# Where experts with several items stand in the loading order of a mixture-of-experts step

## The chip, the cores and the metric

The kernel runs on one core of a Trainium2 chip. The metric is the device time of one execution in microseconds (us), median of three runs. Engines are named as in the profile: PE (TensorE matmul; PEld its weight loads), DVE (VectorE), ACT (ScalarE), POOL (GpSimd), SP (SyncE, which here only issues transfers and waits). SPq marks rows of SP's queue. "L137" is line 137 of the kernel.

## The reference

One decoder layer for 512 prompt tokens and 8 x 4 sample tokens, in float32: an input projection, two mixers (a matrix-memory recurrence and sliding-window attention), a merge, and a hierarchical mixture of experts, then a gated per-layer embedding, each with a layer norm. The change touches only how the experts are scheduled. Cut to that part:

```python
def hier_moe(x, ...):
    g_idx = argmax(x @ w_rg + b_rg)                 # 1 of 4 groups
    top_p, top_i = top_k(softmax(e_logits of that group), 2)   # 2 of its 8 experts
    gate = g_w * top_p / top_p.sum()
    eid = g_idx * 8 + top_i
    y[tok] += gate * (silu(x @ w_gate[eid]) * (x @ w_up[eid])) @ w_down[eid]

x = layer_norm(ALPHA * x + hier_moe(x, ...))
```

There are 32 experts. Each has a gate and an up matrix of 1024 x 512 and a down matrix of 512 x 1024, 2 MiB each, so 6 MiB for one expert. 544 tokens with two experts each make 1088 rows. With the inputs of the reference they fall on 26 of the 32 experts: 230 rows on the fullest, one row on the emptiest.

## The kernel before

**Items and places.** The rows of an expert are cut into items of up to 32 rows. The 26 experts have 49 items: 18 experts have one item, two have 2, three have 3, two have 5 and one has 8. An expert's position in the loading order is its place (0 to 25). PE works through the items in the order of places; SP loads the weights in the same order.

**The order of loading.** It is worked out on the chip, from the counts of rows, by a key for each expert (lines 2037 to 2053); experts are then ranked by the key (lines 2057 to 2080), and the places, the items up to each place and the ends are written to `meta` (L2100). Four experts (ranks 16 to 19 of a list made early from the biases) are loaded before the routing is known; `firsts` holds 32 for them, and their key is about -32, so they take places 0 to 3. Among the other experts in use, `kinds[:, 0]` marks those of exactly one item (S = 14 here) and `kinds[:, 1]` those of more (M = 8 here). `nth` numbers each kind from 1 in the order of the experts' indices. The n-th of the single-item experts has the key n - 0.5; the m-th of the others has the key m x `ratio`, with `ratio` = S / (M + 1) = 14 / 9 = 1.556, which is called the distance here. `ties` adds less than 0.01. An unused expert gets 1000 more.

**Buffers.** There are four slots for weights. Slots 0 and 1 are tiles that the profile calls `w`; slot 2 is `w2a`, `w2b` (the two halves of gate and up) and `w2c`, `w2d` (down); slot 3 is `gu3a`, `gu3b` and `r_p`. Place p uses slot p mod 4 for p up to 23; the last two, 24 and 25, use slots 2 and 3, and slots 0 and 1 are left to what comes behind the experts.

**SP (from L179).** `load_place` (L137, L143) loads a place in six transfers of 1 MiB, in this order: gate and up, first half, when PE has done the first half of gate and up of the last item that uses the slot; gate and up, second half, when PE has done the second half; the two halves of down, when PE has done the down product of that item. SP goes through the places strictly in order, so a wait for one slot holds back all that stands behind it. For places 24 and 25 it waits for places 22 and 23. Behind the experts come the `late` loads (L230): four of 512 KiB (`x1d`) and one of 2 MiB (`w_pg`), which `act` waits for at the end of the phase (semaphore `al`).

**PE (`items_of`).** For each item: 64 matmul instructions for gate and up (L306), in two halves that wait for the two halves of the weights, and then 32 for the down product (L318) of the item before it. So the last down product of a place comes behind the gate and up of the next place. Behind every fourth item PE also turns the next 128 gathered rows (L298). ACT and DVE make silu(gate) x up (L440, L515) and turn it (L479); POOL gathers the rows and scatters the results (L256, L265).

Of the kernel before, what the change touches and what calls it, by code (L numbers as in the profile page):

```python
# [15 lines left out]
ALU = mybir.AluOpType  # L16
# [528 lines left out]
def tile_decoder_step(ctx: ExitStack, tc: tile.TileContext, *aps):  # L545
    nc = tc.nc
    A = dict(zip(_INS + _CONSTS + _OUT_NAMES, aps))
    sy, act, dve, pe, gp = nc.sync, nc.scalar, nc.vector, nc.tensor, nc.gpsimd
# [125 lines left out]
    for pp in range(2):  # L674
        gp.dma_start(
            out=brow[16 + 4 * pp:20 + 4 * pp, :].rearrange("j (a d) -> j a d", a=2),
# [1260 lines left out]
    with ExitStack() as scope:  # L1937
# [26 lines left out]
        def rt(name, shape, dt=F32):  # L1964
            n = -(-count(shape) // 8) * 8
            if dt != F32 or taken[0] + n > arena.shape[1]:
                return R.tile(shape, dt, name=name)
            taken[0] += n
            return view(arena[:, taken[0] - n:taken[0] - n + count(shape)], shape)
# [21 lines left out]
        items, flag, base, key = (rt(n, [P, NEXP]) for n in ("items", "flag", "base", "key"))  # L1991
# [43 lines left out]
        kinds, nth = rt("kinds", [P, 2, NEXP]), rt("nth", [P, 2, NEXP])  # L2035
        ratio = rt("ratio", [P, 1])
# [12 lines left out]
        dve.scalar_tensor_tensor(out=key, in0=nth[:, 0], scalar=-0.5, in1=kinds[:, 0], op0=ALU.add, op1=ALU.mult)  # L2049
        dve.tensor_tensor(out=ratio, in0=ratio, in1=nth[:, 0, NEXP - 1:], op=ALU.mult)  # L2050
        dve.tensor_tensor(out=base, in0=base, in1=key, op=ALU.add)
        dve.scalar_tensor_tensor(out=key, in0=nth[:, 1], scalar=ratio, in1=kinds[:, 1], op0=ALU.mult, op1=ALU.mult)
        dve.tensor_tensor(out=key, in0=key, in1=base, op=ALU.add)

        E = NEXP
        sq, kcol, bcol_ = rt("sq", [E, E]), rt("kcol", [E, 1]), rt("bcol", [E, 1])
# [36 lines left out]
        for n, by, op, m_ in ((80, K["turns"][0:1], ALU.add, 16), (82, iota[0:1, 0:32], ALU.mult, 32)):  # L2093
# [4 lines left out]
                                 op0=ALU.mult, op1=ALU.subtract)  # L2098
# [10 lines left out]
                          in1=hi[:, :, None].to_broadcast([P, 2 * NT5, 20]), op=ALU.is_equal)  # L2109
# [357 lines left out]
```

## Time and profile before

| what | us |
|---|---|
| median of three runs | 1088.85 |
| lowest and highest run | 1086.99, 1091.53 |
| profiled execution, own time | 1091.46 |
| its span (first to last instruction) | 1089.6 |
| PE / DVE / ACT / POOL busy in the span | 995.5 / 510.3 / 367.0 / 253.8 |

The profiled execution lies 2.6 us above the median, and 1.9 us of its time lie outside its span. Up to about 630 us the span holds the projection, the mixers and the merge; the expert phase runs from about 637 to 1012 us; what follows is the tail (second and third norm, gated embedding, outputs). How to read what the prediction quotes: a row of the timeline has start, duration, engine, line, operation, tiles, the count of instructions merged into it, and in brackets the idle time of the engine before it with what ended it. "Issue" there means that the profile shows nothing the engine waited for. A row of the windows has a stretch of the span, its length, the busy time of PE, PEld, DVE, ACT and POOL with the number of instructions, the granted PE clock, the busy share of the 16 DMA engines and the GB/s that they moved.

The items can be counted in the trace: 1408, 384 and 480 instructions of L306 read `w`, `w2a` and `gu3a`. An item has 64 on `w` (both halves of its weights are called so) or 32 on each of `w2a` and `gu3a`, which makes 22 + 12 + 15 = 49 items.

### The profile page before, as it was taken

To read this page: it belongs to the slowest core of one execution; us is meant where nothing else is said; L and a number is where in the kernel's file an instruction comes from. 1 tells how busy PE (TensorE), PEld (TensorE's weight loads), DVE (VectorE), ACT (ScalarE), POOL (GpSimd) and SP (SyncE) were. 2 spreads that over 40 slices of the span, in tenths; PEclk is the share of its full clock that TensorE was granted. 3 is DMA by queue.
4 is the path that set the end of the run, shared out by engine and by line. 5 is a ranking of instruction groups with operands and counts; after the bars stand their busy time and mean duration, and the time that the engine had idled before them with its cause. 6 is when DMAs were issued, how large, how long until landed. Compare 5 with 4: busy or idle time off the path is not lost.

```text
span 1089.6 us, 26983 instructions
## 1 busy us (share of the span) xinstructions
PE 995.5 (91%) x10269; PEld 818.1 (75%) x10270; DVE 510.3 (47%) x1308; ACT 367.0 (34%) x749; POOL 253.8 (23%) x385
## 2 busy tenths in 40 slices
PE   9999999999999999999999976885988788987897
PEld 8988999999988888899989544553556565655675
DVE  5556533635756865664465721211222222223796
ACT  5311223532596784423211311110111111113531
POOL 6000000501445564213410211111222222221011
PEclk9999999999999999999999988999899999999899
DMA  7221322223515432645289989999999999969811
GB/s 260 79 78 42 114 64 67 70 77 96 162 41 151 142 127 98 229 116 151 84 320 381 364 317 409 427 426 426 427 426 426 425 427 426 426 265 420 318 45 63
DMA packets 90892, 256.45 MB, mean 235 GB/s; under 512 B 11115, under 2 KB 58433, under 8 KB 70820
## 3 DMA queue, kind: packets, MB, share of 16 engines
q1 hardware_dynamic: 76036, 224.61, 53.5%
q0 software_dynamic: 10272, 27.21, 6.9%
q10 hardware_dynamic: 4512, 3.64, 1.2%
q8 instruction: 49, 0.80, 0.3%
q14 instruction: 23, 0.19, 0.1%
HBM read 241.89 MB, written 19.61 MB: 240 GB/s over the span
## 4 chain that ended last, share of the span: by engine, by line
PE 49%; issue 6%; DMA 5%; SPq 4%; DVE 3%; ACT 1%; POOL 0%; DVEq 0%; ACTq 0%; POOLq 0%
PE psG L306 14%; PE pj L709 6%; PE kept L318 6%; PE pj L710 6%; PE pj L711 6%; SPq L137 3%; DMA gu3b<-in_w_eu_dram 2%; DMA w<-in_w_pg_dram 2%; PE psX L298 1%; SPq L143 1%; PE po L711 1%; PE sp L1397 1%; PE po L709 1%; PE po L710 1%; PE nm L1385 1%
## 5 line engine op out<-in xcount | busy, mean ns | idle before, releaser
L709 PE MATMUL pj<-xH,wH 128*128 128x256 f32 (+1 forms) x672 | 197.9, 295 | 0.3 <-ACT sigA L879 0.3
L710 PE MATMUL pj<-xL,wH 128*128 128x256 f32 (+1 forms) x672 | 195.9, 292 | 0.0
L711 PE MATMUL pj<-xH,wL 128*128 128x256 f32 (+1 forms) x672 | 194.4, 290 | 0.0
L592 ACT CAST wH<-raw 128x1024 fp32r<-128x1024 f32 x76 | 79.6, 1048 | 192.8 <-PE pj L710 119.0
L709 PEld LDWEIGHTS pj<-xH,wH 128*128 128x128 f32 x672 | 126.5, 188 | 5.9 <-issue 4.4
L711 PEld LDWEIGHTS pj<-xH,wL 128*128 128x128 f32 x672 | 126.4, 188 | 1.4 <-issue 1.2
L710 PEld LDWEIGHTS pj<-xL,wH 128*128 128x128 f32 x672 | 126.4, 188 | 1.3 <-issue 0.8
L593 DVE TENSOR_TENSOR wL<-raw,wH 128x1024 fp32r<-128x1024 f32 x76 | 95.8, 1261 | 66.2 <-ACT wH L592 66.1
L474 DVE COPY xT<-xg 128x256 f32 x48 | 14.5, 302 | 228.4 <-PE psG L306 228.4
L306 PE MATMUL psG<-w,xT 128*32 128x256 f32 x1408 | 89.9, 412 | 31.2 <-issue 30.3
L306 PEld LDWEIGHTS psG<-w,xT 128*32 128x32 f32 x1408 | 55.2, 118 | 63.6 <-issue 44.3
L440 ACT ACTIVATE both<-psG 128x128 f32<-128x128 f32 x49 | 13.6, 278 | 245.5 <-PE psG L306 245.4
L1373 POOL TENSOR_SCALAR lg<-lg,sm 128x256 f32<-128x256 f32 (+1 forms) x64 | 60.0, 951 | 26.2 <-DVE sm L1370 19.9
L265 POOL DMA_INDIRECT ybuf<-ysb,idy x48 | 47.8, 995 | 43.6 <-POOL idy L262 31.6
L426 ACT ACTIVATE xg<-psX,gcol 128x128 f32 (+1 forms) x100 | 36.4, 469 | 50.5 <-PE psX L298 50.5
L709 PE MATMUL pj<-wH,xH 128*128 128x256 f32 x160 | 46.7, 292 | 1.1 <-DVE vs L923 1.0
L318 PE MATMUL kept<-w,hT 128*32 128x256 f32 x704 | 42.5, 379 | 2.5 <-DVE hT L479 2.5
L306 PE MATMUL psG<-gu3a,xT 128*32 128x256 f32 x480 | 30.7, 398 | 15.3 <-issue 6.8
L710 PE MATMUL pj<-wL,xH 128*128 128x256 f32 x160 | 44.3, 277 | 0.0
L711 PE MATMUL pj<-wH,xL 128*128 128x256 f32 x160 | 44.3, 277 | 0.0
L479 DVE STREAM_TRANSPOSE hT<-both 128x128 f32<-128x128 f32 x49 | 20.0, 409 | 44.1 <-PE kept L318 43.8
L253 POOL COPY idx<-tok 128x1 int32 (+1 forms) x12 | 2.2, 185 | 159.4 <-PE psX L298 159.4
(655 smaller groups left out, 2280.8 us busy)
## 6 DMA issues: line engine op xcount, KB each, us to landing
w<-in_w_eg_dram SPq DMA_DIRECT2D x24, 1024.0 KB
w<-in_w_eu_dram SPq DMA_DIRECT2D x24, 1024.0 KB
w<-in_w_ed_dram SPq DMA_DIRECT2D x24, 1024.0 KB
raw<-in_w_in_dram SPq DMA_DIRECT2D x22, 1024.0 KB
r_p<-in_w_ed_dram SPq DMA_DIRECT2D x14, 1024.0 KB, 22.5
w2a<-in_w_eg_dram SPq DMA_DIRECT2D x7, 1024.0 KB
w2a<-in_w_eu_dram SPq DMA_DIRECT2D x7, 1024.0 KB
w2b<-in_w_eg_dram SPq DMA_DIRECT2D x7, 1024.0 KB
```

The lines of the kernel that those rows point to most:

```text
L137: return [eng.dma_start(out=W[s][half][:, i], in_=w[i][bass.ds(e, 1)].rearrange("a (p k) f -> (a p) k f", p=P)[:, ks]) for i in range(2)]
L265: gp.indirect_dma_start(out=ybuf.rearrange("t (q d) -> (t q) d", q=4), out_offset=bass.IndirectOffsetOnAxis(ap=idy[:, r:r + 1], axis=0), i ...
L306: m = pe.matmul(psG[32 * q:32 * q + 32], xT[:, k], W[s][half][:, :, kh, P * q:P * q + P], start=k == 0, stop=k == KD - 1)
L318: m = pe.matmul(out[32 * q:32 * q + 32], hT[:, 32 * k:32 * k + 32], W[s][2][k // 2][:, k % 2, 256 * q:256 * q + 256], start=k == 0, stop=k ...
L426: m = act.activation(out=out, in_=psX[:, k], func=AF.Identity, bias=gcol[:, 1, k:k + 1], scale=gcol[:, 0, k:k + 1])
L479: dve.transpose(out=hT[:].rearrange("p (r t) -> p r t", r=4), in_=h[:].rearrange("p (f r) -> p r f", r=4)).then_inc(S["ch"], 1)
L592: act.copy(out=H, in_=src)
L593: return eng.tensor_tensor(out=L, in0=src, in1=H.bitcast(F32), op=ALU.subtract)
L709: pe.matmul(out, lh(k), rh(k), start=start and i == 0, stop=False)
L710: pe.matmul(out, lh(k), rl(k), start=False, stop=False)
L711: pe.matmul(out, ll(k), rh(k), start=False, stop=stop and i == len(ks) - 1)
L1373: gp.tensor_scalar(out=lg[:, par, j, 0:nk], in0=lg[:, par, j, 0:nk], scalar1=sm[:, 2, par, j:j + 1], scalar2=None, op0=ALU.mult)
```

## The change

```diff
         dve.tensor_tensor(out=base, in0=base, in1=key, op=ALU.add)
-        dve.scalar_tensor_tensor(out=key, in0=nth[:, 1], scalar=ratio, in1=kinds[:, 1], op0=ALU.mult, op1=ALU.mult)
-        dve.tensor_tensor(out=key, in0=key, in1=base, op=ALU.add)
+        dve.scalar_tensor_tensor(out=key, in0=nth[:, 1], scalar=-1.0, in1=kinds[:, 1], op0=ALU.add, op1=ALU.mult)
+        dve.scalar_tensor_tensor(out=key, in0=key, scalar=ratio, in1=base, op0=ALU.mult, op1=ALU.add)
```

The m-th expert of several items gets the key (m - 1) x ratio instead of m x ratio; nothing else changes. With S = 14 and M = 8 the keys of these eight are 0, 1.556, ... 10.889 instead of 1.556, 3.111, ... 12.444, while the single-item experts keep 0.5, 1.5, ... 13.5. The number of items at each place follows from the keys:

| place | 0-3 | 4 | 5 | 6 | 7 | 8 | 9 | 10 | 11 | 12 | 13 | 14 | 15 | 16 | 17 | 18 | 19 | 20 | 21 | 22 | 23 | 24 | 25 |
|---|---|---|---|---|---|---|---|---|---|---|---|---|---|---|---|---|---|---|---|---|---|---|---|
| before | 1 each | 1 | 1 | 2 | 1 | 3 | 1 | 1 | 8 | 1 | 3 | 1 | 1 | 3 | 1 | 5 | 1 | 1 | 5 | 1 | 2 | 1 | 1 |
| after | 1 each | 2 | 1 | 1 | 3 | 1 | 8 | 1 | 1 | 3 | 1 | 3 | 1 | 1 | 5 | 1 | 5 | 1 | 1 | 2 | 1 | 1 | 1 |

The expert of eight items moves from place 11 (slot 3) to place 9 (slot 1), the two of five items from 18 and 21 to 17 and 19, and the last expert of two items from 23 to 22.

## The prediction

> **What bounds the kernel now.** The page's busy times come first, and its rates of transfer (40 slices of 27.2 us).
>
> ```profile
> PE 995.5 (91%) x10269; PEld 818.1 (75%) x10270; DVE 510.3 (47%) x1308; ACT 367.0 (34%) x749; POOL 253.8 (23%) x385
> GB/s 260 79 78 42 114 64 67 70 77 96 162 41 151 142 127 98 229 116 151 84 320 381 364 317 409 427 426 426 427 426 426 425 427 426 426 265 420 318 45 63
> ```
>
> PE is busy 91% of the span, which says little of the expert phase: there (slices 25 to 37) the rate stands at 409 to 427 GB/s, but for one slice of 265. So the windows come next, cut where the rate breaks.
>
> ```profile
> 641.00:957.00 316.00, 255.97 (x4185) 165.97 (x4183) 60.86 (x179) 56.63 (x138) 61.47 (x103) 0.95 1.01 424
> 957.00:969.00 12.00, 10.44 (x184) 6.86 (x187) 2.42 (x8) 4.74 (x11) 4.83 (x8) 1.00 0.27 88
> 969.00:1012.00 43.00, 32.07 (x497) 22.07 (x489) 11.51 (x24) 11.05 (x23) 7.20 (x12) 0.95 0.97 398
> ```
>
> From 641 to 957 us the DMA engines are full (share 1.01, 424 GB/s) while PE is busy 256 of 316 us. From 957 to 969 us they are almost empty (88 GB/s), then full again. At 424 GB/s those 12 us would have carried 12 x (424 - 88) / 424 = **9.5 us** more of transfers. The transfers are the bound of the phase, and this is their one hole. What made it is in SP's timeline, and what ended the phase in the chain of waits.
>
> ```profile
> 788.76 2.06 SPq L143 DMA_DIRECT2D w2d<-in_w_ed_dram  x1
> 808.69 0.33 SPq L137 DMA_DIRECT2D gu3a<-in_w_eg_dram  x1
> ...
> 932.09 1.29 SPq L143 DMA_DIRECT2D r_p<-in_w_ed_dram  x2
> 966.90 0.34 SPq L137 DMA_DIRECT2D w2a<-in_w_eg_dram  x1
> 989.77 0.43 SPq L230 DMA_DIRECT2D w<-in_w_pg_dram  x1
> ```
>
> ```profile
> 738.37 26.51 DMA gu3b<-in_w_eu_dram
> 989.77 21.63 DMA w<-in_w_pg_dram
> ```
>
> Twice SP issued nothing for long: from 791 to 808.7 us, held by the expert of eight items on slot 3, and from 933 to 966.9 us, when place 24 had to wait for place 22 behind the five items of place 21. The first stop left no hole, since transfers issued earlier were still queued: the one issued at 738.37 landed 26.5 us later. The second was longer than that, and the queue ran dry at about 957. Then places 24, 25 and the late loads ran at the full rate until w_pg landed at 989.77 + 21.63 = 1011.4. So the phase ends 1011.4 - 966.9 = 44.5 us after place 24 is issued, and **what sets the end is when PE finishes the first half of gate and up of place 22's last item**. Hence PE's timeline.
>
> ```profile
> 677.74 4.95 PE L306 MATMUL psG<-w,xT 128*32 128x256 f32 x64 [3.57 <-issue]
> 686.58 5.35 PE L306 MATMUL psG<-w,xT 128*32 128x256 f32 x64 [2.17 <-issue]
> ...
> 731.25 3.66 PE L306 MATMUL psG<-w,xT 128*32 128x256 f32 x64
> 738.66 3.66 PE L306 MATMUL psG<-w,xT 128*32 128x256 f32 x64 [2.02 <-issue]
> 745.42 1.93 PE L306 MATMUL psG<-w2a,xT 128*32 128x256 f32 x32 [1.38 <-DMA w2a<-in_w_eu_dram]
> 760.25 3.64 PE L306 MATMUL psG<-gu3a,xT 128*32 128x256 f32 x32 [6.69 <-DMA gu3a<-in_w_eu_dram]
> 771.67 1.93 PE L306 MATMUL psG<-gu3a,xT 128*32 128x256 f32 x32
> 777.41 1.93 PE L306 MATMUL psG<-gu3a,xT 128*32 128x256 f32 x32 [0.35 <-issue]
> 783.06 1.93 PE L306 MATMUL psG<-gu3a,xT 128*32 128x256 f32 x32 [0.27 <-issue]
> ...
> 847.97 1.93 PE L306 MATMUL psG<-gu3a,xT 128*32 128x256 f32 x32 [0.45 <-issue]
> 856.85 5.35 PE L306 MATMUL psG<-w,xT 128*32 128x256 f32 x64 [3.49 <-issue]
> ...
> 908.56 1.93 PE L306 MATMUL psG<-w2a,xT 128*32 128x256 f32 x32 [0.31 <-issue]
> 915.34 1.93 PE L306 MATMUL psG<-gu3a,xT 128*32 128x256 f32 x32 [1.39 <-issue]
> ...
> 957.82 3.66 PE L306 MATMUL psG<-w,xT 128*32 128x256 f32 x64
> 964.77 1.93 PE L306 MATMUL psG<-w2a,xT 128*32 128x256 f32 x32 [1.56 <-issue]
> ```
>
> These give the steps from one item's start to the next: 5.65 us inside a place (777.41 to 783.06, taken as 5.7), 7.4 from slot 0 to 1 (731.25 to 738.66), 6.9 from 1 to 2 (957.82 to 964.77), 6.8 from 2 to 3 (908.56 to 915.34), 8.9 from 3 to 0 (847.97 to 856.85). Every fourth step has one more us for turning rows. Place 10 starts at 745.42 after a wait for its weights, place 11 at 760.25 after another, of 6.69 us. Against the regular steps, 745.42 to 760.25 is 14.8 instead of 6.8, and 760.25 to 771.67 is 11.4 instead of 5.7 + 1.1: PE lost 8.0 + 4.6 = **12.6 us** there, for want of weights, just ahead of the expert that had eight items on one load.
>
> **The change, part by part.** The edit itself replaces one product and one sum by two instructions of the same size.
>
> ```profile
> 620.59 0.25 DVE L2052 SCALAR_TENSOR_TENSOR xg<-nth,ratio,kinds 128x32 f32<-128x32 f32 x1
> 620.87 0.19 DVE L2053 TENSOR_TENSOR xg<-xg 128x32 f32<-128x32 f32 x1
> 625.45 0.27 ACT L2100 CAST meta<-mf 1x96 int32<-1x96 f32 x1
> ```
>
> ```profile
> 623.05 5.73 DMA pld<-ysb
> ```
>
> They took 0.25 and 0.19 us. The new ones work on the same 32 columns, so each takes between the shorter and the longer of these: between -0.06 and +0.06 us for both. `meta` is written by 625.72 us, while the phase starts behind a store of embeddings that lands at 623.05 + 5.73 = 628.78: 3 us of cover, and the edit costs 0 (0.06 us if the cover were gone). No transfer is added or taken away: 22 places behind the four guessed ones, the same gathers and scatters. What moves is which slot is held how long.
>
> *Early: the loads.* Places 10 and 11 were waited for, so their first halves landed at 745.4 and 760.25: 14.8 us for one place. Counted from there, place 9 starts to land at 730.6, place 12 is complete at 760.25 + 14.8 + 9.9 = 785, and the queue would run dry then if place 13 were not issued. After the change place 13 (slot 1) waits for the eight items of place 9. PE begins item 4 at 677.74 as before (the five items up to there are the same) and reaches place 9 eight items later. Before, eight steps took 738.66 - 677.74 = 60.9 us with the same kinds of steps; by the regular ones they take 56 to 58. So place 9 begins at 734 to 739 us, no earlier than its weights land. Its last item begins 7 x 5.7 + 2 x 1.1 = 42.1 us later, at 776 to 781, and its first half is done 1.9 us on: place 13 is issued at 778 to 783, ahead of 785. **No hole opens**, by 2 to 7 us, out of which must come the start of a transfer: estimated at 2 us (966.90 issued, rate back at 969).
>
> *Middle: PE.* PE enters the eight items 21 to 26 us earlier than before, and during these the queue brings places 10 to 12. Places 10 and 11 start at about 784 and 791, their weights (745 and 760) long there. By the same steps PE reaches place 13 at about 818, place 17 at 861 and place 19 at 899; by 14.8 us for a place they have landed whole at 800, 859 and 888. So the 12.6 us of waits go and nothing of their size takes their place; place 17 is the closest.
>
> *Late: the sum.* Place 22 now has two items, so its last item has 45 before it instead of 44, with as many changes of place. SP's clock for place 24: 966.90 + 5.7 (one item) - 12.6 (waits gone) = 960.0. Up to 3 us more come off where the lone items at 677.74 and 686.58 took 4.95 and 5.35 us instead of 3.66, if they run back to back after the change: 957. The queue can't be ahead of about 957.6, where it ran dry before. I take the middle, **958.5**. The rest of the phase follows at the full rate as before: the end moves from 1011.4 to 1011.4 - (966.9 - 958.5) = 1003.0, **8.4 us earlier**, and at most 9.5. PE's own last products, stores and spreads hang on the last weights and move along; the tail of 78 us is the same work.
>
> Against the profiled execution's own time: 1091.46 - 8.4 = 1083.1. That run is 2.6 us above the median of the three; from 1088.85 the forecast is **1080.4 us**.
>
> Here a rule of the Trainium skill bears. The row first: behind the wait of 6.69 us at 760.25 the 32 matmuls took 3.64 us instead of 1.93. The page "TensorE: Matmul & The Clock Gate", in the part on the HAM clock gate, says that PE falls to half its clock after about 3.4 us without work and needs as long of work to come back; the trace agrees at this place. It speaks against a part of the gain, as the second rival below shows.
>
> **The rivals.**
>
> *The waits move instead of going (slower).* If PE is starved as much at places 4 to 9 as it was at 10 and 11, only the extra item of place 22 is left: place 24 is issued at 966.9 + 5.7 = 972.6, the end comes 5.7 us later, 1094.6 us. It decides at 5.7 us regained: with less than that of the 12.6, the kernel is slower. For it: place 9's weights and PE's arrival are within a few us. Against it: the queue up to place 9 is as it was, so that its weights come at 730.6, and eight items behind one load give the next three places 42 us to land. 10% for a change on this side of zero.
>
> *The end turns cold.* Once SP is early, places 24 and 25 come at 14.8 us each while PE needs 7 for one, so PE waits there. The last item's 64 + 32 matmul instructions would then run at the half rate of row 760.25, twice 1.7 us and 1.7 more; on top the spreads behind it.
>
> ```profile
> 1003.29 3.88 PE L150 MATMUL psX<-gb,keep 48*128 48x128 f32 x32
> 1011.81 0.55 PE L150 MATMUL po<-gb,keep 48*128 48x128 f32 x1 [4.64 <-SPq L179]
> ```
>
> PE ended at 1007.2 and idled 4.6 us for w_pg, so 5.1 us of cold work and a cold 3.88 (up to 3.9 more) against 4.6 of cover would cost up to 4.4 us: 1084.8. [...] But that wait existed before in part, and the 3.88 us for 32 of the spreads may be cold already. 10%.
>
> *A hole opens at place 13.* If PE is 5 us late at place 9, the queue is dry for about 3 us at 785 and PE's later clock adds what it is late: the gain shrinks to 3 or 4 us, 1085. 10%.
>
> *Hidden.* Something else ends the phase near 1011 (the x1d loads, the scatters): within 2 us, 1088. For it nothing in the chain, which goes through w_pg. 6%. *The change doesn't do what it says:* rounding in the keys can't, since the nearest keys (0 and 0.5, 1.5 and 1.556) differ by more than `ties`. 2%, at 1089.
>
> **How the numbers follow.** The forecast, 1079 to 1083, has 62%: its lower end is the whole hole of 9.5 us. Cold end and place 13 bring 20% between 1083 and 1087; 18% are nearer to zero or beyond. The three runs lie 1.9 below to 2.7 above their median, so the range of 1077 to 1087 takes in the forecast with 2 us of scatter below and the two partial rivals above. Half a per cent is 5.4 us, about what a measurement of this kernel can tell from no change: faster than 1083.4 has 69%, slower than 1094.3 has 8% (the first rival, most of it), and 23% lie between.
>
> **What would show it.** In PE's timeline: three items on `w` in a row early (places 4 and 5), eight items on `w` from about 737 us, and no waits for transfers of several us between 740 and 900. In SP's: place 13 at 778 to 783, place 24 at 957 to 960, w_pg issued at about 981 and landed at 1003. In the windows: no stretch under 400 GB/s from 641 to 1000. It would be wrong if the rate falls near 785, if places 5 to 9 wait for weights, or if PE ends behind w_pg.

## The result, and the profile after

| | before | after |
|---|---|---|
| median of 22 runs, us | 1092.38 | 1085.39 |
| lowest and highest, us | 1086.99, 1102.58 | 1082.24, 1090.39 |
| span of the profiled execution, us | 1089.6 | 1086.2 |

The ratio of after to before is **0.9931, with a 95% interval of 0.9917 to 0.9945**: 0.69% faster, which at 1092.4 us is 7.5 us (6.0 to 9.1). The medians of the table lie 7.0 us apart, within that interval. The forecast was 8.4 us. The forecast of a time was put on a median 3.5 us lower than this one: 22 runs of the kernel before have 1092.38 us where the first three had 1088.85.

The page of after, with the rows that answer to those of before:

```profile
PE 991.8 (91%) x10269; PEld 819.2 (75%) x10270; DVE 510.1 (47%) x1308; ACT 366.5 (34%) x749; POOL 253.5 (23%) x385
GB/s 246 95 79 39 79 78 78 78 84 63 158 79 104 149 156 99 231 89 136 137 243 403 338 314 389 424 426 427 426 427 426 427 426 425 428 425 412 295 45 64
```

PE is busy nearly as much as before. The single slice of 265 GB/s near the end is gone: from slice 26 to 36 the rate stands at 424 to 428.

In the profiled execution of after, the expert phase starts 3.30 us later than in that of before (first L306 at 642.38 instead of 639.08 us); the work ahead of it is the same. The change does not do this: in the eight other runs, of which e5_lesspg and e6_defer have the order of after too, the phase starts at 638.8 to 639.6 us. So times in the phase are compared from its start, and it ends where SP issues the first load of the tail. The windows of both, in four parts: the first 50 us, the next 250, the stretch from there to 14 us ahead of the end, and the last 14 us. First before, then after.

```profile
639.08:689.08 50.00, 33.78 (x524) 20.84 (x528) 8.80 (x28) 8.36 (x19) 7.45 (x13) 0.91 1.00 410
689.08:939.08 250.00, 207.21 (x3404) 134.86 (x3400) 47.82 (x138) 46.15 (x115) 51.02 (x86) 0.95 1.01 426
939.08:997.78 58.70, 49.82 (x864) 32.71 (x859) 11.97 (x35) 11.88 (x27) 12.53 (x21) 1.00 0.85 351
997.78:1011.78 14.00, 9.39 (x112) 7.26 (x104) 6.19 (x8) 6.03 (x11) 2.31 (x3) 0.87 0.91 364
```

```profile
642.38:692.38 50.00, 34.74 (x524) 21.82 (x528) 8.75 (x28) 8.36 (x19) 6.69 (x13) 0.90 0.98 395
692.38:942.38 250.00, 215.71 (x3696) 144.00 (x3688) 52.01 (x150) 48.16 (x119) 54.60 (x91) 0.99 1.01 426
942.38:994.48 52.10, 35.18 (x572) 22.38 (x567) 7.82 (x22) 9.74 (x23) 9.47 (x16) 0.93 1.01 426
994.48:1008.48 14.00, 9.55 (x116) 7.39 (x109) 6.20 (x8) 6.02 (x11) 2.31 (x3) 0.86 0.77 306
```

The last figure of a row is the rate in GB/s. The full rate is taken as 426.5 (the second part has 426 in both, the page up to 428); what a part falls short of it, times its length, is the time lost to transfers: for the third part of before, 58.7 x (426.5 - 351) / 426.5 = 10.4 us. Part by part before lost 1.9 + 0.3 + 10.4 + 2.1 = 14.7 us of 372.7, and after 3.7 + 0.3 + 0.1 + 4.0 = 8.0 of 366.1 (summed before rounding). **Both leave 358 us: the phase lasts as long as its bytes take at the full rate, plus the time in which too few are asked for.** This is a way to book the time and no proof: what is left is always the bytes moved divided by 426.5 GB/s, and both kernels move the same bytes. That the transfers bound the phase is seen from the rate, which stands at 424 to 428 GB/s in slices 26 to 36 and is higher in no slice of either page, and from the experiments. The stretch ahead of place 24 is gone (10.4 to 0.1). Some 3.7 us of that came back at the two ends of the phase in this pair of executions.

SP's timeline and PE's, after:

```profile
758.45 10.40 SPq L143 DMA_DIRECT2D w<-in_w_ed_dram  x2
783.08 0.33 SPq L137 DMA_DIRECT2D w<-in_w_eg_dram  x1
...
942.74 0.81 SPq L143 DMA_DIRECT2D r_p<-in_w_ed_dram  x2
959.81 0.34 SPq L137 DMA_DIRECT2D w2a<-in_w_eg_dram  x1
...
983.00 2.42 SPq L230 DMA_DIRECT2D w<-in_w_pg_dram  x1
1008.46 0.81 SPq L2245 DMA_DIRECT2D w<-ybuf  x2
```

```profile
983.00 25.09 DMA w<-in_w_pg_dram
```

```profile
642.38 1.93 PE L306 MATMUL psG<-w,xT 128*32 128x256 f32 x32 [0.98 <-DVE xT L493]
...
732.29 3.66 PE L306 MATMUL psG<-w,xT 128*32 128x256 f32 x64 [2.40 <-issue]
739.70 3.66 PE L306 MATMUL psG<-w,xT 128*32 128x256 f32 x64 [2.02 <-issue]
745.24 3.66 PE L306 MATMUL psG<-w,xT 128*32 128x256 f32 x64 [0.16 <-issue]
...
780.90 3.66 PE L306 MATMUL psG<-w,xT 128*32 128x256 f32 x64
...
787.93 1.93 PE L306 MATMUL psG<-w2a,xT 128*32 128x256 f32 x32 [1.64 <-issue]
...
794.55 1.93 PE L306 MATMUL psG<-gu3a,xT 128*32 128x256 f32 x32 [1.23 <-issue]
803.02 5.35 PE L306 MATMUL psG<-w,xT 128*32 128x256 f32 x64 [3.08 <-issue]
...
957.67 1.93 PE L306 MATMUL psG<-w2a,xT 128*32 128x256 f32 x32 [0.16 <-issue]
...
974.72 1.93 PE L306 MATMUL psG<-w2a,xT 128*32 128x256 f32 x32 [0.90 <-issue]
...
987.62 3.49 PE L306 MATMUL psG<-gu3a,xT 128*32 128x256 f32 x32 [8.02 <-DMA gu3a<-in_w_eu_dram]
...
1000.16 3.88 PE L150 MATMUL psX<-gb,keep 48*128 48x128 f32 x32
1008.50 3.75 PE L150 MATMUL po<-gb,keep 48*128 48x128 f32 x16 [4.46 <-SPq L179]
```

The eight items run from 739.70 on, on `w`, and places 10 (787.93) and 11 (794.55) follow at the regular steps of 7.0 and 6.6 us: the waits of 12.6 us are gone. Place 13 is issued at 783.08 and place 24 at 959.81, and SP's pause ahead of place 24 (943.6 to 959.8 us) is 16 us instead of 34. From 692 to 994 us the queue is not dry, so w_pg has more ahead of it: issued at 983.00, it lands 25.1 us later, where before it took 21.6, and holds the tail back until 1008.46.

### The profile page after: what moved, and what is told of

It is laid out like the page before. It is cut to its first block, busy times and chain, and to the rows that moved or that the text cites. A ratio compares the mean times of both kernels' runs of the same rounds, so it can differ in the third digit from the quotient of the medians.

```text
span 1086.2 us, 26979 instructions
## 1 busy us (share of the span) xinstructions
PE 991.8 (91%) x10269; PEld 819.2 (75%) x10270; DVE 510.1 (47%) x1308; ACT 366.5 (34%) x749; POOL 253.5 (23%) x385
## 4 chain that ended last, share of the span: by engine, by line
PE 53%; issue 7%; DMA 3%; DVE 3%; SPq 1%; ACT 1%; POOL 0%; DVEq 0%; ACTq 0%; POOLq 0%
PE psG L306 16%; PE kept L318 8%; PE pj L709 6%; PE pj L710 6%; PE pj L711 6%; DMA w<-in_w_pg_dram 2%; PE psX L298 1%; PE po L711 1%; PE sp L1397 1%; PE po L709 1%; PE po L710 1%; PE nm L1385 1%; SPq L230 1%; PE po L150 1%; DMA pld<-ysb 1%
## 5 line engine op out<-in xcount | busy, mean ns | idle before, releaser
L306 PE MATMUL psG<-w,xT 128*32 128x256 f32 x1664 | 100.4, 395 | 30.5 <-issue 29.5
L306 PEld LDWEIGHTS psG<-w,xT 128*32 128x32 f32 x1664 | 62.5, 114 | 65.4 <-issue 41.8
L1373 POOL TENSOR_SCALAR lg<-lg,sm 128x256 f32<-128x256 f32 (+1 forms) x64 | 60.1, 951 | 26.6 <-DVE sm L1370 20.4
L318 PE MATMUL kept<-w,hT 128*32 128x256 f32 x832 | 50.2, 379 | 2.5 <-DVE hT L479 2.5
L318 PEld LDWEIGHTS kept<-w,hT 128*32 128x32 f32 x832 | 31.4, 110 | 16.1 <-DVE hT L479 2.8
L306 PE MATMUL psG<-gu3a,xT 128*32 128x256 f32 x416 | 26.7, 399 | 16.6 <-issue 8.6
```

The costliest lines, as they stand in the source:

```text
L306: m = pe.matmul(psG[32 * q:32 * q + 32], xT[:, k], W[s][half][:, :, kh, P * q:P * q + P], start=k == 0, stop=k == KD - 1)
L318: m = pe.matmul(out[32 * q:32 * q + 32], hT[:, 32 * k:32 * k + 32], W[s][2][k // 2][:, k % 2, 256 * q:256 * q + 256], start=k == 0, stop=k ...
L1373: gp.tensor_scalar(out=lg[:, par, j, 0:nk], in0=lg[:, par, j, 0:nk], scalar1=sm[:, 2, par, j:j + 1], scalar2=None, op0=ALU.mult)
```

## The experiments

Two theories stood at first. **A:** what counts is how long the expert of eight items holds which slot; moved forward, it takes TensorE's waits away, place 24 is asked for sooner, and the dry stretch closes. **B:** the gain comes from the experts of five items further back. C, D, F, G and H are told with the runs.

**The instructions alone.**

```diff
-scalar=-1.0, in1=kinds[:, 1], op0=ALU.add
+scalar=0.0, in1=kinds[:, 1], op0=ALU.add
```

> The new pair of instructions with a shift of 0, so the order of loading is that of before. Theory A (what counts is which slot the expert of eight items holds, and when: with it moved forward, TensorE no longer waits for weights at places 10 and 11, reaches the end of place 22 sooner, and the transfer queue no longer runs dry ahead of place 24): 1.000 of before, within 0.002, and the stretch of 10 us with few transfers near the end of the phase is still there. Rival D (the instructions, or the order that the compiler gives them, make the difference): some of the 0.7% stays, 0.993 to 0.997.

Measured: 0.9998 (0.9977 to 1.0019). In its phase of 376.8 us 11.9 are lost in the third part. The edit costs nothing that these runs can tell from zero, and D falls: the order of the experts is the effect, to within the 0.2% of this interval.

**Half of the experts, first the early ones, then the late ones.** The shift of one distance is given only to the first four (`is_lt`) or the last four (`is_gt`) experts of several items. The edit in short:

```diff
-key = (nth[:, 1] + -1.0) * kinds[:, 1]
+key = (nth[:, 1] < 4.5) * kinds[:, 1]      # e3_late: > 4.5
+key = nth[:, 1] - key
+key = key * kinds[:, 1]
```

> Only the first four experts of several items move one distance forward (2, 3, 8 and 3 items, so eight items at place 9); the last four keep their places from before, so place 21 has five items, place 22 one and place 23 two. Theory A: the whole gain, 0.993 (0.991 to 0.995); place 24 is issued one item, 5 to 6 us, sooner than after the whole change, but the queue was not dry there any more, so this brings nothing. Rival B (the gain comes from the two experts of five items, which leave places 18 and 21): 1.000. Rival C (TensorE's end of place 22 still sets the end after the change, as the prediction had it): 0.988 to 0.990, since the extra item of place 22 is gone.

Measured: **0.9922 (0.9891 to 0.9953)**, the whole gain. One number of A falls. Place 24 was not issued 5 to 6 us sooner than after the whole change but later, 319.5 us behind the phase's start instead of 317.4, since TensorE, now ahead of the loads, had to wait for them at place 18:

```profile
873.41 1.93 PE L306 MATMUL psG<-w2a,xT 128*32 128x256 f32 x32 [2.23 <-DMA w2a<-in_w_eu_dram]
879.25 3.21 PE L306 MATMUL psG<-w2b,xT 128*32 128x256 f32 x32 [3.91 <-DMA w2b<-in_w_eu_dram]
```

And yet its phase ends at 366.6 us, as the changed kernel's at 366.1. C needed place 24 to come sooner, so this run does not put it to the test, and the interval takes in its 0.990; e4_three decides it below.

> Only the last four experts of several items move one distance forward; the expert of eight items stays at place 11, place 22 has two items. Theory A: TensorE's 12.6 us of waits stay and place 24 is issued one item later than before, so the dry stretch grows by 5 to 6 us: 1.005 (1.003 to 1.007). Rival B: 0.993. Rival D: 0.993 to 0.997.

Measured: **1.0048 (1.0023 to 1.0072)**, slower. TensorE waits at places 10 and 11 as before, and the extra item of place 22 delays place 24:

```profile
761.73 3.64 PE L306 MATMUL psG<-gu3a,xT 128*32 128x256 f32 x32 [5.01 <-DMA gu3a<-in_w_eu_dram]
```

```profile
954.09 0.81 SPq L143 DMA_DIRECT2D r_p<-in_w_ed_dram  x2
970.73 0.34 SPq L137 DMA_DIRECT2D w2a<-in_w_eg_dram  x1
```

```profile
939.32:1003.32 64.00, 46.79 (x736) 29.41 (x731) 9.93 (x29) 10.32 (x25) 10.79 (x18) 0.91 0.84 333
```

The third part loses 64.0 x (426.5 - 333) / 426.5 = 14.0 us where before lost 10.4. B falls: the late half of the change costs by itself, and is carried by the early half.

**How far forward.** Shifts of three, a half and two distances, by the same constant (`scalar=-3.0`, `-0.5`, `-2.0`).

> All eight experts move three distances forward: places 4, 5 and 6 have 2, 3 and 8 items. Theory A: place 10 has to wait for the eight items of place 6, of which the last starts about 75 us behind the first item of place 4; by then the queue has been dry for about 16 us, so the hole near the end is traded for a larger one early: 1.000 to 1.008, with a stretch of 12 to 20 us with few transfers about 105 to 120 us behind the phase's start. Rival F (the further forward, the better, since TensorE has work in hand): 0.993 or less and no such stretch.

Measured: **1.0053 (1.0029 to 1.0077)**, slower. The eight items at place 6 hold up place 10:

```profile
717.98 0.81 SPq L143 DMA_DIRECT2D w<-in_w_ed_dram  x2
755.87 0.33 SPq L137 DMA_DIRECT2D w2a<-in_w_eg_dram  x1
```

```profile
739.00:757.00 18.00, 17.34 (x305) 11.38 (x301) 4.23 (x12) 5.01 (x12) 4.92 (x9) 1.00 0.17 52
```

From 718.8 to 755.9 us SP issues nothing, 37 us, which is longer than the queue lasts, and from 739 to 757 us there are 52 GB/s: 18.0 x (426.5 - 52) / 426.5 = 15.8 us lost, 100 us behind the phase's start. Nothing is lost ahead of place 24. F falls: forward helps only up to where the hole opens early instead. C falls here too:

```profile
959.31 0.34 SPq L137 DMA_DIRECT2D w2a<-in_w_eg_dram  x1
1019.29 0.81 SPq L2245 DMA_DIRECT2D w<-ybuf  x2
```

Place 24 is issued 320.3 us behind the phase's start (639.04), 7.5 us sooner than before, and yet the phase ends 7.5 us later than before, 60 us behind that issue: where the queue is not dry, the moment of place 24 does not set the end.

> All eight experts move half a distance forward: the eight items stand at place 10, place 23 has two items again counted from the order 1 2 1 3 1 1 8 1 3 1 1 3 1 1 5 1 5 1 1 2 1 1 of places 4 to 25. Theory A: TensorE loses one place's wait instead of two, place 24 is issued some 2 to 4 us behind where the queue runs dry: 0.993 to 0.997, with a smaller hole near the end. Rival F (the further forward, the better): between 1.000 and 0.993 as well, so this run only gives the dose.

Measured: 0.9939 (0.9915 to 0.9963); 2.0 us are still lost ahead of the end.

> All eight move two distances forward: eight items at place 8 (slot 0), so place 12 waits for them. Theory A: by the steps of the trace before, the last of the eight is through its first half about 94 us behind the first item of place 4 while the queue has work for 92 us, so a hole of 2 to 5 us opens there and the one near the end is gone: 0.993 to 1.000. Rival F: 0.990 or less.

Measured: 0.9952 (0.9927 to 0.9976); 2.6 us are lost between 50 and 300 us, and none ahead of place 24. Half, one and two distances can't be told from each other by their intervals; nought and three can be told from all of them, nought from two only just (0.9977 against 0.9976). So, as far as these runs tell, the dose has a flat bottom between the two holes.

**Fewer bytes.**

```diff
-[(*pg_half(0), "al")]
+[(*(v[:, 0:1] for v in pg_half(0)), "al")]
```

> The order after the change; of the last load of the phase (w_pg, 2 MiB) only 256 KiB are loaded, so the gate of the embedding is computed from wrong weights. Theory A, put sharper (the phase lasts as long as its bytes take at the full rate, plus the time in which the queue is dry): 1.75 MiB less are 1.84 MB / 426 GB/s = 4.3 us less, down to where TensorE's own end takes over (it ended 4.1 us ahead of this load): 3 to 4.3 us below the changed kernel, 0.989 to 0.991 of before. Rival G (TensorE's chain sets the end, the load of w_pg only happens to land with it): as the changed kernel, 0.993.

Measured: 0.9905 (0.9869 to 0.9942), whose interval takes in both theories. The trace tells more: the phase takes 363.5 us, 2.6 less than that of the changed kernel. The bytes left out are worth 4.3 us; the end moved less because another chain took over:

```profile
997.22 4.63 DVE w L538 x4
```

```profile
1002.61 3.75 PE po L150 x16
```

DVE's four products on the residual rows (L538) come behind the last expert's sum, run until 997.22 + 4.63 = 1001.85 us, and PE's first product of the tail follows at 1002.61: they now end the phase. In the changed kernel these products end at 1000.88 + 4.62 = 1005.50 us, 2.6 us ahead of w_pg, which lands at 983.00 + 25.09 = 1008.09:

```profile
1000.88 4.62 DVE L538 TENSOR_TENSOR w<-w,r_s 128x1024 f32<-128x1024 f32 x4
```

So the traces say that w_pg sets the end, against G, and that 2.6 us were to be had from it. The times do not confirm this by themselves, and the phases of the four faster runs with all their bytes end between 364.6 and 366.6 us, a scatter of nearly the same size.

**The down loads later.** SP issues gate and up of place p and then the down loads of place p - 1. The edit in short:

```diff
     gate and up of (s, p)
-    wait dn; load_dn(s, p)
+    if a > 1 or s > 0: wait dn; load_dn(s - 1, p - 1)
...
+load_down(NB - 1, turns * NB - 1)    # behind the loop
```

> The order after the change, and SP issues the two down loads of a place behind the gate and up loads of the next place, so that a wait for a down product no longer holds back the next gate and up. Theory A: the queue's short dry stretch about 30 us behind the phase's start (0.7 to 1.7 us of transfers lost in the traces so far, 2 to 4 with the start of the phase) goes, nothing else changes: 1 to 2 us below the changed kernel, 0.991 to 0.993 of before, a few TensorE waits of one or two us in other places. Rival H (that stretch is lost to the start of the gathers, not to SP's order): 0.993 and the stretch stays.

Measured: **1.0026 (1.0002 to 1.005)**: the change's gain is gone, a miss. H stays open: from 30 to 35 us behind the phase's start the rate is 411 GB/s (292 in after), but it is 400 to 419 in before, e3_late, e4_three, e7_half and e8_two too, which keep SP's order. What took the gain is elsewhere: the second item of a place now waits for its first item's down weights:

```profile
709.01 1.93 PE L319 MATMUL psG<-gu3a,xT 128*32 128x256 f32 x32 [0.16 <-issue]
721.79 2.02 PE L319 MATMUL psG<-gu3a,xT 128*32 128x256 f32 x32
...
745.46 3.66 PE L319 MATMUL psG<-w,xT 128*32 128x256 f32 x64 [0.16 <-issue]
753.46 3.66 PE L319 MATMUL psG<-w,xT 128*32 128x256 f32 x64 [0.80 <-issue]
```

```profile
776.00:790.00 14.00, 12.46 (x214) 7.79 (x204) 3.62 (x10) 4.74 (x11) 3.43 (x6) 1.00 0.63 243
```

The steps inside places 7 and 9 are 12.8 and 8.0 us instead of 5.7 (6.8 with the turning of rows). So the eight items end later, place 13 is issued later, and a hole opens at 776 us: 14 x (426.5 - 243) / 426.5 = 6.0 us. Another 3.1 us are lost ahead of place 24.

The ten phases, by the same windows:

| | ratio | end, us | lost: 0-50 | 50-300 | 300 to 14 ahead of end | last 14 | end less lost |
|---|---|---|---|---|---|---|---|
| before | 1 | 372.7 | 1.9 | 0.3 | 10.4 | 2.1 | 358.0 |
| after | 0.9931 | 366.1 | 3.7 | 0.3 | 0.1 | 4.0 | 358.1 |
| e1_null | 0.9998 | 376.8 | 3.9 | 0.3 | 11.9 | 2.6 | 358.1 |
| e2_early | 0.9922 | 366.6 | 4.4 | 0.3 | 0.4 | 3.1 | 358.4 |
| e3_late | 1.0048 | 378.0 | 3.0 | 0.3 | 14.0 | 2.5 | 358.1 |
| e4_three | 1.0053 | 380.2 | 1.3 | 17.3 | 0.0 | 2.9 | 358.7 |
| e5_lesspg | 0.9905 | 363.5 | 4.7 | 0.3 | 0.1 | 4.5 | 353.9 |
| e6_defer | 1.0026 | 373.0 | 2.9 | 6.2 | 3.1 | 2.6 | 358.3 |
| e7_half | 0.9939 | 365.3 | 2.8 | 0.3 | 2.0 | 2.3 | 358.0 |
| e8_two | 0.9952 | 364.6 | 1.0 | 2.6 | 0.0 | 2.4 | 358.6 |

No version was found that is clearly faster than the changed kernel: e2_early and e5_lesspg lie below it, one within its interval and the other with work left out.

## Why the prediction was right

What the change does was foreseen; the time was met with some luck. The forecast stood on a median of 1088.85 us. On the 1092.38 of 22 runs it would be 1084.0, so 3.5 us of the distance to the measured 1085.39 lie in the kernel before and 1.4 in the gain. The time fell above the 1079 to 1083 that had 62%, into the part of the range kept for a cold end that costs and for a hole at place 13, and neither came.

Taken from the phase's start (3.30 us off its times after), step by step:

- *What bounds it:* right. The rate of the second part is 426 GB/s in all seven traces in which no hole opens there. The order of the experts that closes the late hole, or most of it, without opening a large one makes the kernel 0.5 to 0.8% faster (after, e2_early, e7_half, e8_two), one that widens it or trades it for a larger one 0.5% slower (e3_late, e4_three). That the nine phases with all their bytes come to 358.0 to 358.7 us behind their losses follows from the booking. It was not "their one hole", as the sum below shows.
- *The edit:* 0 as said, to within 0.2% (e1_null).
- *Early, the loads:* place 9 was forecast for 734 to 739 us and came at 736.4; place 13 for 778 to 783, and was issued at 779.8. No hole opened.
- *Middle, PE:* the 12.6 us of waits went, and no wait of their size came before place 25.
- *Late, the sum:* place 24 was forecast for 958.5 and came at 956.5. The size is what was off, and the step is "The rest of the phase follows at the full rate as before". The 44.5 us from place 24 to w_pg (44.9 to the tail's first load) hold only where the queue is dry when place 24 is asked for. After, it wasn't, and 48.7 us passed to the tail's first load. The ceiling of 9.5 us treated that stretch as the one hole; but before also lost 1.9 and 2.1 us at the ends of the phase, and after 3.7 and 4.0, so the traced gain is 10.3 - 1.8 - 1.9 = 6.6 us. Two errors worked against each other: place 24 came 2.0 us sooner than forecast, and the stretch behind it took 3.8 us longer. Over 22 runs the gain is 7.5.
- *The waits move (slower):* not so in the whole change, but e3_late is this rival made real: with the waits kept and the extra item of place 22, 1.0048.
- *The cold end:* the wait came, 8 us ahead of 987.62, and 32 matmuls took 3.49 us instead of 1.93, as the rule of the Trainium skill cited in the prediction says ("TensorE: Matmul & The Clock Gate", the HAM clock gate). Of the 5.1 us of cold work that this rival counted, 1.6 came: the 64 matmuls behind these ran at 1.9 to 2.1 us for 32. It cost nothing: PE ended its phase at 1004.0 and idled 4.5 us for w_pg. The wait need not be as long as that rule's 3.4 us, though: at 803.02 the 64 matmuls took 5.35 us instead of 3.66 behind 3.08 us without work, with a granted clock of 0.52 from 803 to 805 us.
- *A hole at place 13:* not after one distance, but e8_two shows a small one (2.6 us), where place 12 has to wait for the eight items, and e4_three the full one.
- *Hidden, and the change doesn't do what it says:* neither. The chain still goes through w_pg, and the next chain ends 2.6 us ahead of it (e5_lesspg). PE's rows have the items at the places that the keys give.
- *A sign that failed:* "no stretch under 400 GB/s from 641 to 1000". The first 50 us moved 395; the last section tells what goes with it.

## What to carry to other kernels

Where weights stream through a ring of buffers at the full rate of transfers, order the work so that a long stay in one buffer comes when several others are still to be filled, and check both ends: too late and the stream dries up near the end, too early and it dries up at once. Count it in bytes at the full rate plus the time in which the queue is dry; the moment of one issue sets the end only while the queue is dry at that moment. And a wait that an in-order issuer meets is worth moving only if what is moved with it isn't needed sooner.

## What the runs showed of the hardware

The first 50 us of the phase lost between 1.0 and 4.7 us from one execution to the next, 1.9 and 3.9 us with the same order (before, e1_null). It goes with the moment at which SP issues the down loads of place 5, which wait for the down product of place 1: issued 30.0 to 31.3 us behind the phase's start, 3.7 to 4.7 us were lost (after, e1_null, e2_early, e5_lesspg); issued 26.6 to 28.2 us behind it, 1.0 to 3.0 (before, e3_late, e4_three, e7_half, e8_two). That product comes behind the matmuls of places 0 to 2, some of which ran at about half the rate in some executions. Here place 2, in after and in e8_two:

```profile
664.02 3.64 PE L306 MATMUL psG<-w2a,xT 128*32 128x256 f32 x32 [5.78 <-issue]
667.40 3.19 PE L306 MATMUL psG<-w2b,xT 128*32 128x256 f32 x32
```

```profile
660.10 1.93 PE L306 MATMUL psG<-w2a,xT 128*32 128x256 f32 x32 [3.47 <-issue]
661.83 1.94 PE L306 MATMUL psG<-w2b,xT 128*32 128x256 f32 x32
```

Place 2 is not all of it: e3_late and e7_half have it at the full rate and lost 3.0 and 2.8 us, and there the first 32 matmuls of place 0 took 3.39 and 3.35 us instead of 1.93. That the slow matmuls are the cause was not tried by itself.

The last bytes do not end at once. After a long stretch at the full rate the last 14 us lost 4.0 and 4.5 us (after, e5_lesspg), where a hole had been passed shortly before 2.1 to 2.6 (before, e1_null, e3_late, e6_defer, e7_half); e2_early, e4_three and e8_two, without a late hole, lie at 3.1, 2.9 and 2.4. What makes the difference was not tried, and stays open.
